# Layer 1's queries as three groups of block products, a product behind each stage of a head, and weights' sums by adding transfers

## The chip, the cores and the metric

The kernel runs on one NeuronCore of a Trainium2 chip. The metric is device time in microseconds, the median of three runs: 1967.92 us for the kernel before (1966.67 to 1968.24). All timelines below are of one profiled execution.

## What is computed

512 tokens of width 1024 pass two layers, each a gated feed-forward (width 2816), a mixer and a second feed-forward. Layer 0's mixer is a gated causal convolution of width 3 beside four heads of attention to 256 memory tokens; layer 1's is eight heads of causal attention with forget gates (the fox heads) beside four memory heads. All is float32. The lines of the reference that the change bears on are these:

```python
proj = h @ a_w_in[i]                      # layer 0: gates, u and qm
qm = proj[..., 3 * CONV_DIM:].reshape(b, s, MEM_HEADS, MEM_HEAD_DIM)
y_mem = memory_attention(qm, mk, mv)
x = x + jnp.concatenate([y_tok, y_mem], axis=-1) @ a_w_out[i]
...
proj = h @ b_w_q[j]                       # layer 1: q and qm, 12 tiles of 128 columns
q = proj[..., :FOX_WIDTH].reshape(b, s, FOX_HEADS, FOX_HEAD_DIM)
qm = proj[..., FOX_WIDTH:].reshape(b, s, MEM_HEADS, MEM_HEAD_DIM)
y_tok = forgetting_attention(q, k_sh, v_sh, c_sh)
y_mem = memory_attention(qm, mk, mv)
```

`memory_attention` is a softmax of q k / sqrt(128) over 256 memory tokens, times v.

## The kernel before

Activations lie transposed, as eight tiles of 128 features by 512 tokens. A float32 product is made of three TensorE products of rounded halves (`mm3`, L223, L226, L227): each operand is split into a high part `hi` (ScalarE, a copy that rounds, L129 for weights and L231 for activations) and a low part `lo` (VectorE, the rest, L130 and L232).

**Two ways to multiply.** A plain projection (`project`) makes one tile of 128 outputs with 8 x 3 matmuls of 512 columns. A block product group (`group`) takes a 2 x 2 block of weights (two output tiles by two halves of the inputs, each block 512 x 256) and of activations (feature halves by token halves; `Quad` makes the combinations of activations that it needs) and makes four output tiles with seven products instead of eight. Each product is 24 matmuls of 256 columns that accumulate in a PSUM bank. The products are called B11, T1, T2, B21, T3, B22 and T4; `Rows` takes their results apart into tiles. A group whose input statistics are still under way is called with `first`, and makes these statistics behind its second product.

**The weights** are one stream of units in program order (`Weights`, `W`). A unit is 128 x 1024: loaded eight units ahead on SyncE's queue (SP), split two units ahead, and used once. A block of seven units is made from five raw tiles, since three of its units are sums of blocks: raw[4] = a21 + a22 and raw[3] = a11 + a21 are loaded with a second, accumulating load on GpSimd's queue (POOL, L100), and raw[0] += raw[4] and raw[1] += raw[0] are made in place on VectorE (L138) behind the splits of the second and the fourth unit. PIECE says which raw tile each unit reads. Raw tiles lie in 5 buffers `wr` and 3 buffers `ws`, split ones in 4 `wh` and 4 `wl`.

**The mixers.** In layer 0 the four memory heads' queries are one group (`first`), and then the convolution's first three groups are drawn, two products at a time, beside the stages of the heads: `scores` (TensorE, reductions on VectorE, exponentials on ScalarE, `normalise` on VectorE), `turn` (eight transposes on TensorE, then splits) and `values`. In layer 1 each of the twelve query tiles is a plain projection, drawn by `pipeline` three heads ahead, the fox heads' first four beside the memory heads and the other four behind the out-projection. PSUM has eight banks: four `mm`, three `seeded` and one `aux`; while `spread` is set, which it is throughout layer 1's mixer, plain tiles rotate through seven.

**What sets the order.** A scheduler orders the instructions of each engine when the program is built, by its own estimates of durations and by priorities in program order; each engine then runs its own in that fixed order. Loads on SP stand in the order that the code writes. An instruction that waits holds up all behind it on its engine.

Of the kernel before, what the change touches and what calls it, by code (L numbers as in the profile page):

```python
# [12 lines left out]
ALU = mybir.AluOpType  # L13
# [15 lines left out]
MH = 4  # L29
# [10 lines left out]
class Weights:  # L40
# [5 lines left out]


    LOAD, SPLIT = 8, 2

# [15 lines left out]

    def block(self, ap):

        w = ap.shape[1] // 4
        item = {"ap": [ap[:, i * w : (i + 1) * w] for i in range(4)], "w": w, "raw": [None] * 5}
        self.units += [(item, q) for q in range(7)]  # L70
# [42 lines left out]
    def begin(self):  # L113

        i = self.split
        self.split += 1
        item, q = self.units[i]
        self.load_to(i + 1)
        if q is None:
            step, raw, w = item["step"], item["raw"], item["ap"].shape[1]  # L120
        else:
            step = w = item["w"]
            raw = item["raw"][self.PIECE[q]]
        hi, lo = self.tile("wh", F32R), self.tile("wl", F32R)
        self.parts[i] = (hi, lo)
        for a in range(0, w, step):
            c = slice(a, min(a + step, w))
            yield (
                self.nc.scalar.activation(hi[:, c], raw[:, c], AF.Copy),  # L129
                self.nc.vector.tensor_tensor(  # L130
                    out=lo[:, c], in0=raw[:, c], in1=hi[:, c].bitcast(F32), op=ALU.subtract
                ),
            )

        for at, to, of in ((1, 0, 4), (3, 1, 0)):
            if q == at:
                r = item["raw"]
                self.nc.vector.tensor_tensor(out=r[to][:, :w], in0=r[to][:, :w], in1=r[of][:, :w], op=ALU.add)  # L138
# [13 lines left out]
def model(ctx: ExitStack, tc: tile.TileContext, A, out):  # L152
# [45 lines left out]

    def bank(tag="mm"):
        if tag == "mm" and spread[0]:  # L200
            tag = ["mm"] * 4 + ["seeded"] * 3
            tag = tag[taken[0] % 7]
            taken[0] += 1
        return ppool.tile([P, T], F32, tag=tag, name=name(tag), bufs=BANKS[tag])

    def prime(x):

        spread[0] = False
        for b in [bank("seeded") for _ in range(BANKS["seeded"])]:
# [157 lines left out]
    chunks(A["mkv"][1])  # L367
    plan_ffn(0)
    for i in range(4):
        W.block(A["ain"][i])  # L370
    chunks(A["wout"][0, :2])
# [4 lines left out]
    plan_ffn(2)  # L376
    chunks(A["wqm"])
    chunks(A["wq"][:2])
    chunks(A["wout"][1, :2])
    chunks(A["wq"][2:])  # L380
    W.add(A["wf"], (KD * NH,))
# [172 lines left out]
    def ffn(n, x, quads, st, cols, last=None, begin=None):  # L554


        nst, nxt = Stats(), [c() for c in cols]
        new = list(x)
        hid = {}
        def halves(t):  # L560
# [88 lines left out]
    class OutProj:  # L649
# [7 lines left out]
        def run(self, d, upto, ahead=Weights.SPLIT):  # L657
# [4 lines left out]
            if d not in self.ps:  # L662
                self.ps[d] = bank()
            for k in range(self.done[d], upto):
# [209 lines left out]

    def queries(q, nd, st):

        wait = []

        def project_(h):
            wait.append((h, project(nd, mid=st.step1 if h == 1 else None)))  # L880
            if h:
                for i, ps in wait:
                    q[i] = scaled(ps, SCALE, st.row)
                wait.clear()

        return project_

    X0 = [keep(x) for x in X]
    store(KD)
    q, ym, yt, acc, gc = {}, {}, [None] * KD, {}, {}  # L890

    def query(row, i, t):
        q[2 * row + i] = parts()
        split(t, *q[2 * row + i])

# [39 lines left out]
    def gated(ch):  # L935
        def done(row, i, t):
            yt[ch + 2 * row + i] = parts()
            split(t, *yt[ch + 2 * row + i])

        return Rows(done, lambda row, i: acc[ch + 2 * row + i])  # L940

# [15 lines left out]

    for _ in group(quads.quads, Rows(query, lambda row, i: st.row, SCALE), begin):
        pass
    more = channels(0)  # L960

    def products(n):
        for _ in range(n):
            next(more)


    products(2)
    for i in range(MH + 2):
        if i >= 2:
            values(i - 2)  # L970
        if 0 < i <= MH:
            turn(i - 1)
        if i < MH:
            scores(i)
        products(2)
    for _ in more:
        pass
    X = [x() for x in X0]
# [8 lines left out]
    store(KD)  # L987
    X, st, (nd,) = ffn(2, X, quads.quads, st2, [lambda: Normed(V_MIX + 8)])

    spread[0] = True  # L990

    q, ym, Q, kvn = {}, {}, {}, Normed(V_KV)

    def fox_query():
        Q[len(Q)] = scaled(project(nd), SCALE, st.row)

    pipeline(MH, 3, queries(q, nd, st), *mem_heads(q, *mem_back(1), ym), [fox_query] * 4)
    for k in range(KD):
        kvn.add(k, X0[k]("t"))
    OutProj(X, ym, MH).finish()  # L1000
    for _ in range(4):
        fox_query()

# [229 lines left out]
def laid_out(a):  # L1233
# [55 lines left out]
    for c in (0, 4):  # L1289
        rows += [(8 + c, 16 + c), (10 + c, 18 + c), (c, c + 2)]  # L1290
    r0, r1 = (t[[i for r in rows for i in (r[h], r[h] + 1)]] for h in range(2))
    g["ain"] = blocks(
        *(two(v, 0) for v in (r0[:, :, :KP], r0[:, :, KP:], r1[:, :, KP:], r1[:, :, :KP]))
    )

# [8 lines left out]
    tk, tq = tiles(kvf[:, :D]), tiles(a["b_w_q"][0])  # L1304
    g["wqm"] = pairs(tq[NH:], 2)
    g["wk"], g["wq"] = pairs(tk, 2), pairs(tq[:NH], 2)
    vec = np.zeros((P, NVEC), f)
# [37 lines left out]
```

## Time and profile before

| what | value |
|---|---|
| median of three runs | 1967.92 us (1966.67 to 1968.24) |
| the profiled execution's time | 1968.88 us |
| its span | 1967.1 us, mean granted clock 0.995 |
| layer 0's query group, first part | 411.6 to 436 us |
| layer 0's heads with products beside them | 436 to 486 us |
| layer 1's entry, its memory heads | 1330 us, 1340 to 1382 us |
| VectorE in-place sums L138 | 102 in the whole kernel, 1.22 us each |

The page gives for each engine its busy time, and for groups of instructions the line, the engine, output and input tiles, their count, busy time and mean; a row of the timeline gives the start and the duration in us, and in square brackets how long the engine had been idle and what released it. `<-` points from the output to its inputs. The lines that matter stand in the prediction.

### The profile page before, as it was taken

Reading aid. Unit: us, or ns where it says so; the run is one execution under the profiler, and the core shown is the slowest. Engines: PE = TensorE matmul, PEld = TensorE weight load, DVE = VectorE, ACT = ScalarE, POOL = GpSimd, SP = SyncE. Lnnn points to the kernel's source line nnn. Section 1 sums busy time; section 2 is a strip of 40 time slices with the busy share of each in tenths; the row PEclk is TensorE's granted clock in tenths of the full one; section 3 lists DMA queues with packets and bytes.
Section 4 is the critical chain, followed back from the end, with each engine's and each line's share of the span. In section 5 each row is a group of like instructions: output and inputs, shape, how many; then the busy total and the mean of one; then the engine's idle time right before and its main releaser. Section 6 shows DMA issues by size and latency. Waiting matters only on the chain.

```text
span 1967.1 us, 31607 instructions
## 1 busy us (share of the span) xinstructions
PE 1942.0 (99%) x12845; PEld 1786.9 (91%) x12845; DVE 1437.4 (73%) x1998; ACT 976.5 (50%) x1434; POOL 102.8 (5%) x138
## 2 busy tenths in 40 slices
PE   8899999999999999999999999999999999999998
PEld 7899999999998998989899898988878889989896
DVE  7976667798787975767887576777546688757674
ACT  7653444566455652535565253545335575525353
POOL 0000000000000000000000000000001100000000
PEclk9899999999999999999999999999999999999999
DMA  8875566665664673657467365432322237637441
GB/s 294 229 218 154 135 158 153 176 170 142 183 177 123 165 197 100 173 138 181 150 177 190 97 174 140 131 127 96 127 93 69 76 98 194 192 100 179 131 116 43
DMA packets 89010, 293.32 MB, mean 149 GB/s; under 512 B 10016, under 2 KB 12192, under 8 KB 88864
## 3 DMA queue, kind: packets, MB, share of 16 engines
q1 hardware_dynamic: 74176, 237.82, 37.1%
q0 software_dynamic: 14688, 53.48, 17.0%
q8 instruction: 100, 1.64, 0.3%
q14 instruction: 46, 0.38, 0.1%
HBM read 280.78 MB, written 10.49 MB: 148 GB/s over the span
## 4 chain that ended last, share of the span: by engine, by line
PE 95%; DVE 3%; ACT 1%; DMA 1%; issue 1%; SPq 0%; DVEq 0%; ACTq 0%
PE mm L223 19%; PE mm L226 19%; PE mm L227 19%; PE seeded L223 12%; PE seeded L227 12%; PE seeded L226 12%; DMA wr<-in_mkv 1%; DVE wl L130 1%; DVE s L232 0%; ACT wh L129 0%; PE mm L1118 0%; DVE t L251 0%; DVE wr L138 0%; PE seeded L1118 0%; PE mm L756 0%
## 5 line engine op out<-in xcount | busy, mean ns | idle before, releaser
L129 ACT ACTIVATE wh<-wr 128x1024 fp32r<-128x1024 f32 (+2 forms) x422 | 437.0, 1038 | 699.5 <-PE mm L226 352.8
L223 PE MATMUL mm<-s,wh 128*128 128x256 f32 (+1 forms) x2236 | 734.3, 329 | 1.1 <-ACT s L235 1.1
L226 PE MATMUL mm<-s,wh 128*128 128x256 f32 (+1 forms) x2236 | 734.4, 328 | 0.7 <-DVE s L232 0.5
L227 PE MATMUL mm<-s,wl 128*128 128x256 f32 (+1 forms) x2236 | 733.7, 328 | 0.9 <-DVE wl L130 0.8
L130 DVE TENSOR_TENSOR wl<-wr,wh 128x1024 fp32r<-128x1024 f32 (+2 forms) x422 | 503.4, 1194 | 173.9 <-ACT wh L129 172.2
L223 PE MATMUL seeded<-s,wh 128*128 128x256 f32 (+1 forms) x1748 | 507.3, 290 | 0.3 <-ACT t L454 0.3
L227 PE MATMUL seeded<-s,wl 128*128 128x256 f32 (+1 forms) x1748 | 506.2, 290 | 0.0
L226 PE MATMUL seeded<-s,wh 128*128 128x256 f32 (+1 forms) x1748 | 506.1, 290 | 0.0
L223 PEld LDWEIGHTS mm<-s,wh 128*128 128x128 f32 x2236 | 426.3, 191 | 38.7 <-ACT s L235 1.8
L226 PEld LDWEIGHTS mm<-s,wh 128*128 128x128 f32 x2236 | 426.3, 191 | 38.6 <-DVE s L232 1.3
L227 PEld LDWEIGHTS mm<-s,wl 128*128 128x128 f32 x2236 | 426.2, 191 | 38.2 <-DVE wl L130 1.3
L223 PEld LDWEIGHTS seeded<-s,wh 128*128 128x128 f32 x1748 | 335.1, 192 | 4.8 <-ACT t L454 0.5
L227 PEld LDWEIGHTS seeded<-s,wl 128*128 128x128 f32 x1748 | 335.1, 192 | 4.4
L226 PEld LDWEIGHTS seeded<-s,wh 128*128 128x128 f32 x1748 | 335.1, 192 | 4.1
L628 DVE SCALAR_TENSOR_TENSOR t<-mm,r 128x512 f32<-128x512 f32 x96 | 66.1, 688 | 172.3 <-PE mm L227 172.3
L129 ACT ACTIVATE wh<-ws 128x1024 fp32r<-128x1024 f32 x102 | 108.2, 1061 | 137.3 <-PE mm L226 59.2
L100 POOL DMA_DIRECT2D ws<-in_gu x88 | 76.5, 870 | 1237.0 <-DMA ws<-in_gu 337.6
L232 DVE TENSOR_TENSOR s<-t,s 128x512 fp32r<-128x512 f32 (+1 forms) x204 | 126.7, 632 | 4.1 <-ACT s L231 4.0
L130 DVE TENSOR_TENSOR wl<-ws,wh 128x1024 fp32r<-128x1024 f32 x102 | 124.2, 1218 | 1.3 <-ACT wh L129 0.5
L231 ACT ACTIVATE s<-t 128x512 fp32r<-128x512 f32 (+1 forms) x204 | 112.4, 577 | 14.9 <-DVE t L306 7.8
L457 DVE TENSOR_TENSOR t<-seeded,t 128x512 f32<-128x512 f32 x94 | 64.7, 688 | 36.3 <-PE seeded L227 36.2
L631 DVE TENSOR_TENSOR s<-s,t 128x512 f32<-128x512 f32 (+1 forms) x97 | 66.4, 685 | 2.6
(183 smaller groups left out, 1412.1 us busy)
## 6 DMA issues: line engine op xcount, KB each, us to landing
wr<-in_gu SPq DMA_DIRECT2D x132, 512.0 KB, 4.0
ws<-in_gu SPq DMA_DIRECT2D x88, 512.0 KB, 4.5
ws<-in_gu POOLq DMA_DIRECT2D x88, 512.0 KB, 6.3
wr<-in_dn SPq DMA_DIRECT2D x64, 512.0 KB, 4.4
wr<-in_dn SPq DMA_DIRECT2D x32, 384.0 KB, 4.0
wr<-in_wout SPq DMA_DIRECT2D x24, 512.0 KB, 4.4
wr<-in_ain SPq DMA_DIRECT2D x21, 512.0 KB, 4.9
kept<-s SPq DMA_DIRECT2D x32, 256.0 KB, 3.1
```

The costliest lines, as they stand in the source:

```text
L100: self.nc.gpsimd.dma_start(out=t[:, :w], in_=more, accum_op=ALU.add)
L129: self.nc.scalar.activation(hi[:, c], raw[:, c], AF.Copy),
L130: self.nc.vector.tensor_tensor(out=lo[:, c], in0=raw[:, c], in1=hi[:, c].bitcast(F32), op=ALU.subtract),
L223: i = nc.tensor.matmul(ps, wh, xh, start=first, stop=more, skip_group_check=more)
L226: nc.tensor.matmul(ps, wh, xl, start=False, stop=more, skip_group_check=more)
L227: nc.tensor.matmul(ps, wl, xh, start=False, stop=last or more, skip_group_check=more)
L231: nc.scalar.activation(hi, src, AF.Copy)
L232: nc.vector.tensor_tensor(out=lo, in0=src, in1=hi.bitcast(F32), op=ALU.subtract)
L457: nc.vector.tensor_tensor(out=out, in0=a, in1=b, op=ALU.add)
L628: nc.vector.scalar_tensor_tensor(out=t[:, c], in0=ps[:, c], scalar=-0.5, in1=st.row[:, c], op0=ALU.mult, op1=ALU.mult)
L631: nc.vector.tensor_tensor(out=y[:, c], in0=y[:, c], in1=t[:, c], op=ALU.add)
```

## The change

Four things change.

1. Layer 1's twelve query tiles become three block groups (`g["bin"]`, in the order memory heads, fox heads 0 to 3, fox heads 4 to 7). Feed-forward 2 ends in `Quads` instead of `Normed`; the first group makes the statistics. X is stored (`X1`) and loaded again behind the groups, as in layer 0, and the inputs of keys and values are loaded (`kvn`) there too. All queries come ahead of the out-projection. The out-projection's tiles stay on the four `mm` banks, also where it is continued late in the mixer; `spread` is set only behind layer 1's memory heads.
2. Both mixers draw products beside the heads by one new function, `beside`, one product between stages.
3. The second and the third block of each mixer (`moved`) have their two sums made by adding transfers from SBUF to SBUF on POOL's queue, issued behind the splits of the first and the fourth unit.
4. Small shared helpers (`head`, `by_rows`) take the place of repeated code.

```diff
-    def block(self, ap):
+    def block(self, ap, moved=False):
...
+        r = item["raw"]
+        for at, to, of in ((0, 0, 4), (3, 1, 0)) if item["moved"] else ((1, 0, 4), (3, 1, 0)):
+            if q == at and item["moved"]:
+                self.nc.gpsimd.dma_start(out=r[to][:, :w], in_=r[of][:, :w], accum_op=ALU.add)
+            elif q == at:
                 self.nc.vector.tensor_tensor(out=r[to][:, :w], in0=r[to][:, :w], in1=r[of][:, :w], op=ALU.add)
...
-    def bank(tag="mm"):
-        if tag == "mm" and spread[0]:
-            tag = ["mm"] * 4 + ["seeded"] * 3
-            tag = tag[taken[0] % 7]
+    def bank(tag=None):
+        if tag is None:
+            tag = "seeded" if spread[0] and taken[0] % 7 > 3 else "mm"
             taken[0] += 1
...
     for i in range(4):
-        W.block(A["ain"][i])
+        W.block(A["ain"][i], i in (1, 2))
...
-    chunks(A["wqm"])
-    chunks(A["wq"][:2])
+    for i in range(3):
+        W.block(A["bin"][i], i in (1, 2))
     chunks(A["wout"][1, :2])
-    chunks(A["wq"][2:])
...
-                self.ps[d] = bank()
+                self.ps[d] = bank("mm")
...
+    def head(t, q, h):
+        q[h] = parts()
+        split(t, *q[h])
+
+    def queries(quads, st, q, first):
+
+        done = lambda row, i, t: head(t, q, 2 * row + i)
+        for _ in group(quads, Rows(done, lambda row, i: st.row, SCALE), first):
+            pass
+
+    def beside(more, scores, turn, values):
+        def products(n):
+            for _ in range(n):
+                next(more, None)
+
+        products(1)
+        scores(0)
+        products(2)
+        for h in range(MH):
+            turn(h)
+            if h + 1 < MH:
+                products(1)
+                scores(h + 1)
+                products(1)
+                values(h)
+                products(1)
+            else:
+                products(2)
+                values(h)
+        for _ in more:
+            pass
...
-    for _ in group(quads.quads, Rows(query, lambda row, i: st.row, SCALE), begin):
-        pass
-    more = channels(0)
-
-    def products(n):
-        for _ in range(n):
-            next(more)
-
-    products(2)
-    for i in range(MH + 2):
-        if i >= 2:
-            values(i - 2)
-        if 0 < i <= MH:
-            turn(i - 1)
-        if i < MH:
-            scores(i)
-        products(2)
-    for _ in more:
-        pass
+    queries(quads.quads, st, q, begin)
+    beside(channels(0), scores, turn, values)
...
-    X, st, (nd,) = ffn(2, X, quads.quads, st2, [lambda: Normed(V_MIX + 8)])
+    X, st, (quads,) = ffn(2, X, quads.quads, st2, [lambda: Quads(V_MIX + 8)])
+
+    X1 = [keep(x) for x in X]
+    store(KD)
+    q, ym, Q, kvn = {}, {}, {}, Normed(V_KV)
+
+    def fox_queries():
+        for h in (0, MH):
+            done = lambda row, i, t: head(t, Q, h + 2 * row + i)
+            g = group(quads.quads, Rows(done, lambda row, i: st.row, SCALE))
+            for _ in UNITS:
+                next(g, None)
+                yield
+
+    stages = mem_heads(q, *mem_back(1), ym)
+    queries(quads.quads, st, q, st.step1)
+    beside(fox_queries(), *stages)
+    X = [x() for x in X1]
+    for k in range(KD):
+        kvn.add(k, X0[k]())
+    OutProj(X, ym, MH).finish()
 
     spread[0] = True
-
-    q, ym, Q, kvn = {}, {}, {}, Normed(V_KV)
-
-    def fox_query():
-        Q[len(Q)] = scaled(project(nd), SCALE, st.row)
-
-    pipeline(MH, 3, queries(q, nd, st), *mem_heads(q, *mem_back(1), ym), [fox_query] * 4)
-    for k in range(KD):
-        kvn.add(k, X0[k]("t"))
-    OutProj(X, ym, MH).finish()
-    for _ in range(4):
-        fox_query()
```

Line numbers of the changed kernel are a little higher: the splits of weights are L130 and L131, the accumulating load L101, the adding transfer L141, the copies L457, the exponentials L749.

**Place one: POOL in layer 0's mixer.** In the kernel before, the accumulating loads of the convolution's blocks follow one another (ws339 and ws348 are of the second block in the stream, ws358 and ws367 of the third, ws377 of the fourth):

```order
L100 DMA ws339_4313<-in_ain 128x1024
L100 DMA ws348_4478<-in_ain 128x1024
L100 DMA ws358_4636<-in_ain 128x1024
L100 DMA ws367_4774<-in_ain 128x1024
L100 DMA ws377_5011<-in_ain 128x1024
L100 DMA ws386_5183<-in_ain 128x1024
```

In the changed kernel, the same place reads:

```order
L101 DMA ws339_4313<-in_ain 128x1024
L101 DMA ws348_4478<-in_ain 128x1024
L101 DMA ws358_4636<-in_ain 128x1024
L141 DMA wr340_4316<-ws339_4313 128x1024
L101 DMA ws367_4774<-in_ain 128x1024
L141 DMA wr345_4436<-wr340_4316 128x1024
L101 DMA ws377_4981<-in_ain 128x1024
L141 DMA wr359_4639<-ws358_4636 128x1024
L101 DMA ws386_5153<-in_ain 128x1024
L141 DMA wr364_4742<-wr359_4639 128x1024
```

Each sum of a moved block (wr340, wr345, then wr359, wr364) stands behind an accumulating load of a later tile. In layer 1's mixer the first two sums likewise stand behind a load each (ws1089, ws1098).

**Place two: ScalarE in the same stretch.** wh360 is the split of the second block's summed unit (raw wr340, for its third product), wh365 and wh368 are later units, s_ are splits of the query tiles, and the exponentials belong to head 0. Before:

```order
L129 ACTIVATE wh360_4676<-wr340_4316 128x1024
L231 ACTIVATE s_427_4622<-t_422_4551 128x512
L129 ACTIVATE wh362_4707<-wr345_4436 128x1024
L454 ACTIVATE seeded_436_4704<-mm_435_4675 128x512
L231 ACTIVATE s_429_4627<-t_423_4553 128x512
L129 ACTIVATE wh365_4770<-ws348_4478 128x1024
L231 ACTIVATE s_431_4666<-t_425_4587 128x512
L454 ACTIVATE t_438_4738<-mm_437_4706 128x512
L231 ACTIVATE s_433_4671<-t_426_4589 128x512
L129 ACTIVATE wh368_4803<-wr345_4436 128x1024
L745 ACT_TABLE_LOAD
L745 ACTIVATE t_442_4743,su_440_4741<-mm_441_4742,nm_439_4740 128x256 x2
```

After:

```order
L130 ACTIVATE wh360_4676<-wr340_4316 128x1024
L234 ACTIVATE s_429_4628<-t_423_4553 128x512
L130 ACTIVATE wh362_4737<-wr345_4436 128x1024
L234 ACTIVATE s_431_4666<-t_425_4587 128x512
L457 ACTIVATE seeded_436_4704<-mm_435_4675 128x512
L130 ACTIVATE wh365_4770<-ws348_4478 128x1024
L234 ACTIVATE s_433_4671<-t_426_4589 128x512
L749 ACT_TABLE_LOAD
L749 ACTIVATE t_440_4709,su_438_4707<-mm_439_4708,nm_437_4706 128x256 x2
L749 ACTIVATE t_442_4718,su_438_4707<-mm_441_4717,nm_437_4706 128x256 x2
L457 ACTIVATE t_445_4768<-mm_444_4736 128x512
L457 ACTIVATE seeded_446_4801<-seeded_436_4704 128x512
```

The summed unit's split keeps its place, but reads what POOL's transfer leaves; the copy `seeded_436` of the first product's result stands one split later, and wh368, the unit of the second sum, has moved from ahead of head 0's exponentials to behind them.

**Place three: VectorE in the same stretch.** wl361 and wl369 are the low parts of the two summed units, nm_ the reductions of head 0's scores, rs_ and the two rows behind it its normalising, and s_449 the low part of head 0's turned tile. Before:

```order
L130 TENSOR_TENSOR wl363_4708<-wr345_4436,wh362_4707 128x1024
L232 TENSOR_TENSOR s_430_4628<-t_423_4553,s_429_4627 128x512
L138 TENSOR_TENSOR wr345_4436<-wr345_4436,wr340_4316 128x1024
L232 TENSOR_TENSOR s_432_4667<-t_425_4587,s_431_4666 128x512
L740 TENSOR_REDUCE nm_439_4740<-mm_441_4742 128x2
L232 TENSOR_TENSOR s_434_4672<-t_426_4589,s_433_4671 128x512
L740 TENSOR_REDUCE nm_439_4740<-mm_443_4751 128x2
L130 TENSOR_TENSOR wl366_4771<-ws348_4478,wh365_4770 128x1024
L130 TENSOR_TENSOR wl369_4804<-wr345_4436,wh368_4803 128x1024
L721 RECIPROCAL rs_445_4764<-su_440_4741 128x4
L723 TENSOR_SCALAR t_442_4743<-t_442_4743,rs_445_4764 128x256 x2
L723 TENSOR_SCALAR t_444_4752<-t_444_4752,rs_445_4764 128x256 x2
```

After:

```order
L744 TENSOR_REDUCE nm_437_4706<-mm_439_4708 128x2
L235 TENSOR_TENSOR s_432_4667<-t_425_4587,s_431_4666 128x512
L744 TENSOR_REDUCE nm_437_4706<-mm_441_4717 128x2
L131 TENSOR_TENSOR wl363_4738<-wr345_4436,wh362_4737 128x1024
L235 TENSOR_TENSOR s_434_4672<-t_426_4589,s_433_4671 128x512
L131 TENSOR_TENSOR wl366_4771<-ws348_4478,wh365_4770 128x1024
L725 RECIPROCAL rs_443_4730<-su_438_4707 128x4
L727 TENSOR_SCALAR t_440_4709<-t_440_4709,rs_443_4730 128x256 x2
L727 TENSOR_SCALAR t_442_4718<-t_442_4718,rs_443_4730 128x256 x2
L131 TENSOR_TENSOR wl369_4822<-wr345_4436,wh368_4821 128x1024
L235 TENSOR_TENSOR s_449_4809<-mm_447_4803,s_448_4808 128x512
```

The sum L138 is gone from between the query tiles' splits, and wl369 has moved from ahead of head 0's normalising to between it and the split of the turned tile.

More of the change, by code (lines that the diff above doesn't have):

```diff
@@ L64, in add @@
         assert at == ap.shape[1]
-    def block(self, ap):
+    def block(self, ap, moved=False):
         w = ap.shape[1] // 4
-        item = {"ap": [ap[:, i * w : (i + 1) * w] for i in range(4)], "w": w, "raw": [None] * 5}
+        item = {"ap": [ap[:, i * w : (i + 1) * w] for i in range(4)], "w": w, "raw": [None] * 5, "moved": moved}
         self.units += [(item, q) for q in range(7)]
@@ L133, in begin @@
             )
-        for at, to, of in ((1, 0, 4), (3, 1, 0)):
-            if q == at:
-                r = item["raw"]
+        if q is None:
+            return
+        r = item["raw"]
[3 more added lines that the diff above has]
+            elif q == at:
                 self.nc.vector.tensor_tensor(out=r[to][:, :w], in0=r[to][:, :w], in1=r[of][:, :w], op=ALU.add)
@@ L206, in prime @@
     def prime(x):
-        spread[0] = False
         for b in [bank("seeded") for _ in range(BANKS["seeded"])]:
@@ L558, in ffn @@
         new = list(x)
+        spread[0] = False
         hid = {}
@@ L872, in model @@
     )
[L875 to L886, printed above, removed]
+    def head(t, q, h):
[25 more added lines that the diff above has]
+            pass
     X0 = [keep(x) for x in X]
@@ L890, in model @@
     q, ym, yt, acc, gc = {}, {}, [None] * KD, {}, {}
-    def query(row, i, t):
-        q[2 * row + i] = parts()
-        split(t, *q[2 * row + i])
     r2 = small.tile([P, T], F32, tag="r2", name="r2", bufs=1)
@@ L935, in gated @@
     def gated(ch):
[L936 to L940, printed above, removed]
+        return Rows(lambda row, i, t: head(t, yt, ch + 2 * row + i), lambda row, i: acc[ch + 2 * row + i])
     def channels(ch):
@@ L1290, in laid_out, with by_rows @@
         rows += [(8 + c, 16 + c), (10 + c, 18 + c), (c, c + 2)]
[L1291 to L1294, printed above, removed]
+    def by_rows(t, rows):
+        r0, r1 = (t[[i for r in rows for i in (r[h], r[h] + 1)]] for h in range(2))
+        return blocks(
+            *(two(v, 0) for v in (r0[:, :, :KP], r0[:, :, KP:], r1[:, :, KP:], r1[:, :, :KP]))
+        )
+    g["ain"] = by_rows(t, rows)
     def outw(w):
@@ L1304, in laid_out @@
     tk, tq = tiles(kvf[:, :D]), tiles(a["b_w_q"][0])
-    g["wqm"] = pairs(tq[NH:], 2)
-    g["wk"], g["wq"] = pairs(tk, 2), pairs(tq[:NH], 2)
+    g["wk"] = pairs(tk, 2)
+    g["bin"] = by_rows(tq, [(8, 10), (0, 2), (4, 6)])
     vec = np.zeros((P, NVEC), f)
```

## The prediction

> **What bounds the kernel now.** The page comes first: one core, its span, what each engine is busy, and the chain of work that ended last.
>
> ```profile
> span 1967.1 us, 31607 instructions
> PE 1942.0 (99%) x12845; PEld 1786.9 (91%) x12845; DVE 1437.4 (73%) x1998; ACT 976.5 (50%) x1434; POOL 102.8 (5%) x138
> PE 95%; DVE 3%; ACT 1%; DMA 1%; issue 1%; SPq 0%; DVEq 0%; ACTq 0%
> ```
>
> TensorE is the bound: a matmul less is worth its issue interval, and every other engine matters only where TensorE waits for it. So the second view is that of TensorE's waits, and the third the busy time in the stretches that the change touches: layer 0's group and heads (436 to 486), the two stage entries (985, 1330) and layer 1's heads (1340).
>
> ```profile
> PE aux L261 <- ACT t L231: 6.4, 1, 6.4
> PE mm L223 <- DVE s L232: 1.7, 2, 1.4
> ...
> 411.60:436.00 24.40, 24.16 (x196) 23.48 (x195) 24.19 (x37) 15.82 (x22) 0.86 (x1) 1.00 0.78 229
> 436.00:468.00 32.00, 30.61 (x246) 29.71 (x245) 30.93 (x52) 24.94 (x54) 2.60 (x3) 1.00 0.62 146
> 468.00:486.40 18.40, 18.11 (x127) 17.12 (x126) 15.30 (x26) 9.85 (x20) 0.88 (x1) 0.91 0.53 136
> 985.00:1005.00 20.00, 19.76 (x159) 19.08 (x158) 20.00 (x29) 14.42 (x19) 0.86 (x1) 1.00 0.58 155
> 1330.00:1340.00 10.00, 10.00 (x45) 8.23 (x45) 8.33 (x10) 4.27 (x6) 0.00 (x0) 1.00 0.46 163
> 1340.00:1382.00 42.00, 42.00 (x226) 36.06 (x225) 29.84 (x55) 23.69 (x56) 0.00 (x0) 1.00 0.26 87
> ```
>
> The columns after the stretch are PE, PEld, DVE, ACT, POOL, then the granted clock. Layer 1's heads lose nothing today: TensorE is busy 42.00 of 42.00 us. Layer 0's lose 1.39 us (30.61 of 32.00) in a single gap, and VectorE has almost no slack there (24.19 of 24.40, then 30.93 of 32.00).
>
> **What goes, and what comes for it.** Layer 1's twelve query tiles are plain projections today, each 8 x 3 matmuls of 512 columns. Two starts of such matmuls that lie ten apart, and then the first 256-column matmuls of two products in a row (24 apart):
>
> ```profile
> 1327.79 0.39 PE L226 MATMUL mm<-s,wh 128*128 128x512 f32 x1
> ...
> 1330.06 0.40 PE L227 MATMUL mm<-s,wl 128*128 128x512 f32 x1
> ...
> 440.31 0.28 PE L223 MATMUL seeded<-s,wh 128*128 128x256 f32 x1
> ...
> 443.19 0.28 PE L223 MATMUL mm<-s,wh 128*128 128x256 f32 x1
> ```
>
> From start to start that is 2.27 / 10 = 0.227 us and 2.88 / 24 = 0.120 us. So 12 x 24 x 0.227 = 65.3 us goes, and 3 groups x 7 products x 24 x 0.120 = 60.5 us comes: **-4.8 us**. Its entry takes the form that layer 0's and the feed-forward stages' entries have, whose rows above show 0.24 us idle each (24.16 of 24.40, 19.76 of 20.00) where layer 1's shows none: **+0.2**.
>
> In layer 0 the products are spread out so that one stands behind each stage of a head. The gap of 1.39 us stood before the scores of a head, with the turn directly ahead of it:
>
> ```profile
> 465.07 1.04 PE L756 MATMUL mm<-cst,t 128*128 128x128 f32 x8
> 467.50 0.38 PE L223 MATMUL mm<-s,s 128*128 128x256 f32 x1 [1.39 <-DVE s L232]
> ```
>
> In the new order a product stands between a turn and the next scores, so this wait has 2.9 us of cover. With it goes the lowered clock behind it (0.91 over 18.4 us: 18.4 x 0.09 = 1.7 us). **-3.1**.
>
> A sentence of the Trainium skill stands against that last figure: "TensorE: Matmul & The Clock Gate" (Why this matters for your kernels) puts the harm to the clock at idle gaps over about 3 us; by it the 1.39 us gap would have cost no clock, and the change would get 1.4 here rather than 3.1. The row with 0.91 disagrees with the page, and the measurement decides.
>
> Without any new wait the sum is 1968.9 - 4.8 + 0.2 - 3.1 = **1961.2** on the profiled execution's scale (1968.88 us for a span of 1967.1), about 1 less on the scale of the median.
>
> **The sums by adding transfers.** A group needs two sums of raw weights, r0+=r4 and then r1+=r0. Today VectorE makes them (L138), and in the second and third group of each mixer an accumulating transfer on POOL's queue does now. VectorE is relieved of 8 x 1.2 us. The price is latency, and here are the rows for it: the sum in layer 0's second group and what stands around it, on VectorE, POOL and ScalarE.
>
> ```profile
> L138 DVE TENSOR_TENSOR wr<-wr,ws 128x1024 f32<-128x1024 f32 x51 | 62.4, 1224 | 1.4
> ...
> 428.38 1.22 DVE L130 TENSOR_TENSOR wl<-wr,wh 128x1024 fp32r<-128x1024 f32 x1
> 432.53 1.22 DVE L138 TENSOR_TENSOR wr<-wr,ws 128x1024 f32<-128x1024 f32 x1
> ...
> 429.45 0.86 POOL L100 DMA_DIRECT2D ws<-in_ain  x1 [20.64 <-DMA ws<-in_ain]
> ...
> 433.86 1.06 ACT L129 ACTIVATE wh<-wr 128x1024 fp32r<-128x1024 f32 x1 [4.52 <-DVE wr L138]
> 436.29 0.58 ACT L454 ACTIVATE seeded<-mm 128x512 f32<-128x512 f32 x1
> 441.15 1.28 ACT L745 ACT_TABLE_LOAD   x1
> 442.45 0.47 ACT L745 ACTIVATE t<-mm,nm 128x256 f32<-128x256 f32 x1
> ...
> 444.63 1.14 DVE L723 TENSOR_SCALAR t<-t,rs 128x256 f32<-128x256 f32 x4
> ```
>
> The sum must not start before the first unit's split has read r0 (VectorE, 428.38 + 1.1 = 429.5). On POOL it stands directly behind the next group's accumulating load, which is at 429.45 and leaves POOL free at 430.31. So the transfer is issued at about 430.3 where VectorE's sum was ready at 433.66: it has 3.4 us. No row shows an accumulating transfer within SBUF. The nearest are the accumulating loads of the same 512 KB: the one at 429.45, then two issued 1.2 us apart, alone by the first and then the second.
>
> ```profile
> ws<-in_ain POOLq DMA_DIRECT2D x1, 512.0 KB, 6.3
> ...
> ws<-in_gu POOLq DMA_DIRECT2D x1, 512.0 KB, 6.1
> ...
> ws<-in_gu POOLq DMA_DIRECT2D x1, 512.0 KB, 8.4
> ```
>
> The second one takes 8.4 us because it queues behind the first. The new sum is issued 0.9 us behind another accumulating load, which is that case, so I take 8.4: it lands at L = 430.3 + 8.4 = **438.7**. The bounds are 433.7 (as ready as now) and 438.7; alone it would be 436.6.
>
> By a page of the Trainium skill it would be the low end: "DMA: Bandwidth & Descriptors" (Anatomy of one DMA, SWDGE path) fits 2.0 us + bytes/436e3 per us, that is an estimate of 3.2 us for 512 KB, a landing at 433.5 and no wait. The trace's 6.1 to 8.4 us for accumulating loads of that size disagree with the fit.
>
> What L does is seen from ScalarE's order: the split of the summed unit stands ahead of another split, of the copy that product 3 accumulates onto, and of head 0's exponentials; all of them wait with it. From the rows: split to end of copy is 433.86 to 436.87, 3.0 us, and one more 512-column split (0.5) now lies between, so product 3 can start at L + 3.5 = 442.2, where TensorE wants it at 440.31. Head 0's normalised exponentials come after one more weight split and one more split (1.5), the table load, exponentials and normalising (441.15 to 445.77, 4.6): L + 9.6 = 448.3. TensorE wants the turn at 443.19. So it is 5.1 late.
>
> The second sum (r1+=r0) waits for VectorE's split of the summed r0, which stands behind two splits and two reductions: about L + 5.7. It also has another accumulating load ahead of it on POOL, so again 8.4: L2 = L + 14.1 = 452.8. In VectorE's order its unit's split (0.95 on ScalarE, 1.1 on VectorE) stands ahead of the split of head 0's turned tile, and the second half of head 1's scores takes that tile's bank: possible at L2 + 2.75 = 455.6. TensorE without waits is there at 443.19 + 0.86 (turn) + 2.88 (product) + 0.72 (half the scores) = 447.65. So by then the layer is **7.9 us** late, the 5.1 included. Layer 1 has the same orders, load and sum adjacent on POOL included: **+8**. The third group's sums follow half a stage later; between 0 and 2.9 for layer 0, where the fourth sum has a load ahead of it, and 0 to 0.5 for layer 1, taken as 2 together. Sum: 7.9 + 8 + 2 = **+18**.
>
> **Smaller edits.** Feed-forward 2's last downs make operands of block products where they made normalised tiles, as feed-forwards 0 and 1 do without loss. X is stored and fetched again, and the inputs of keys and values are fetched later: -0 to +3, taken as 0. The out-projection keeps to four banks, so the last head's turned tiles share one: 0 to +3, taken as 0. Layer 1's VectorE work grows to about that of layer 0's heads (30.93 of 32.00), but the eight sums are gone from it: 0 to +2, taken as 0.
>
> **Rivals.** (a) *The transfer is quick*: within SBUF it lands by about 434, all waits above vanish, and the sum is 1961.2, that is **1960** as a median: faster. It turns on this one latency: below 3.4 us no wait, and above, each us costs about one in each layer. For it: nothing is fetched from HBM. Against it: the nearest rows take 6.1 or more. This is also what the fit on the Trainium skill's page "DMA: Bandwidth & Descriptors" would give. (b) *Not queued but alone*: 6.3 us for each of the two, so L = 436.6, L2 = L + 12 = 448.6, and the scores' bank is free at 451.4: 3.7 us late per layer; 1961.2 + 7.5 + 1 = 1969.7, **1969** as a median: no difference. (c) *The waits add up*: the third group's too (+3.4), a lowered clock behind each long wait (0.09 over 18 us, 1.7 us twice), and the tail's banks (+3): 1961.2 + 16 + 3.4 + 3.4 + 3 = **1987**. (d) *It doesn't do what it says*: relieved or not, VectorE stays as busy, and layer 0 keeps its 3.1 us; that adds 3 to each case above (1981 to the forecast, 1963 to (a)) and changes no sign, so it has no chance of its own.
>
> **How the numbers follow.** The forecast: 1961.2 + 18 = 1979.2, on the median's scale **1978**, chance 0.44; (c) 0.18; (b) and its neighbourhood 0.16; (a) 0.22. The range 1960 to 1988 takes in all of them save the ends, the forecast's own range is 1972 to 1983. About 0.2%, 3.9 us, is what a measurement of this kernel can tell from no change. Faster by more (below 1964.0): 0.22, that is (a). Within: 0.14, most of (b). Slower (above 1971.9): 0.64.
>
> **What would show it.** In the profile of the changed kernel: the adding transfers' time to landing (6 to 8 us right, under 4 wrong); TensorE's waits for the exponentials' normalising before head 0's turn and for VectorE's split before head 1's scores, some 8 us in each mixer; ScalarE idle at the summed unit's split with the transfer as releaser; the 1.39 us wait gone. A transfer of 3 us, or TensorE busy throughout both mixers, would make the prediction wrong, and so would sums that another order on ScalarE lets pass.

## The result, and the profile after

The changed kernel takes **1983.91 us** (median, 1980.87 to 1985.33), the kernel before 1967.99 in the same session: 1.0081 times as long, 95% interval 1.0069 to 1.0093. It is slower, by 15.9 us. The profiled execution of the changed kernel took 1984.88 us. Of its page, the span, the engines' busy time and the chain that ended last by engine:

```profile
span 1983.1 us, 32232 instructions
...
PE 1942.6 (98%) x13061; PEld 1795.3 (91%) x13061; DVE 1459.0 (74%) x2053; ACT 998.0 (50%) x1472; POOL 114.9 (6%) x152
...
PE 88%; DVE 5%; DMA 3%; issue 2%; ACT 1%; SPq 0%; DVEq 0%; ACTq 0%; POOL 0%; POOLq 0%
```

The view of TensorE's waits (source, total us, times, longest):

```profile
PE mm L226 <- DVE s L235: 9.8, 4, 3.4
PE aux L264 <- ACT t L234: 6.4, 1, 6.4
PE mm L760 <- DVE t L727: 4.6, 2, 2.3
```

TensorE's share of the chain that ended last fell from 95% to 88%, and transfers and VectorE took it over. Of the waits, the 6.4 us one is from the start of the kernel and was there before; the first row was 1.7 us and the third is new. In layer 0 they stand where the prediction put them, in the timeline of TensorE (start, duration, instruction, idle time before it and its releaser):

```profile
441.34 0.39 PE L226 MATMUL seeded<-s,wh 128*128 128x256 f32 x1 [0.99 <-ACT seeded L457]
...
446.77 1.25 PE L760 MATMUL mm<-cst,t 128*128 128x128 f32 x8 [2.29 <-DVE t L727]
...
454.97 0.39 PE L226 MATMUL mm<-s,s 128*128 128x256 f32 x1 [3.38 <-DVE s L235]
```

These are product three, head 0's turn, and the second half of head 1's scores: 0.99 + 2.29 + 3.38 = 6.7 us. The last head's scores wait another 1.28 us. What made these three late is read from the chain of waits in the same stretch (start, duration, what), here without its short issue steps:

```profile
421.32 7.16 DMA ws<-in_ain
...
429.83 7.82 DMA wr<-ws
...
437.75 1.07 ACT wh L130
...
438.85 1.22 DVE wl L131
440.07 0.60 DVE s L235
440.67 0.60 DVE nm L744
441.27 0.60 DVE s L235
441.87 0.60 DVE nm L744
442.47 1.13 DVE wl L131
443.60 0.61 DVE s L235
444.22 7.76 DMA wr<-wr
...
452.00 1.06 ACT wh L130
```

TensorE is not in it at all. The path is a load, the first sum's transfer, the split of the summed unit on ScalarE and VectorE, VectorE's queue up to the split of the next unit, the second sum's transfer, and its split again. Each of these two transfers takes 7.8 us where VectorE's add took 1.2. The waits also cost clock; the windows (TensorE, its loads, VectorE, ScalarE and POOL busy, then the granted clock) show 0.93 and 0.92 behind them in the two mixers:

```profile
444.00:470.00 26.00, 20.33 (x150) 19.51 (x150) 16.03 (x29) 14.68 (x34) 2.62 (x3) 0.93 0.75 181
1384.00:1405.00 21.00, 18.13 (x133) 17.57 (x132) 15.11 (x28) 14.48 (x34) 0.86 (x1) 0.92 0.28 77
```

That is about 26 x 0.07 + 21 x 0.08 = 3.5 us on top of the idle time. Narrower windows show that each of the two is a single stretch of 3.4 us at half the clock, and that the 0.91 of the kernel before, which the prediction read over 18.4 us, is one such stretch too (first the kernel before, then the changed one, each time with the 3.4 us ahead of it):

```profile
465.82:469.24 3.42, 1.74 (x13) 1.30 (x12) 3.42 (x7) 1.63 (x4) 0.00 (x0) 1.00 0.59 157
469.24:472.65 3.41, 3.41 (x17) 3.18 (x16) 3.41 (x6) 2.11 (x9) 0.00 (x0) 0.50 0.07 24
...
452.29:455.71 3.42, 0.74 (x6) 0.74 (x7) 2.62 (x3) 3.42 (x5) 0.88 (x1) 1.00 0.76 183
455.71:459.12 3.41, 3.41 (x19) 3.41 (x18) 3.27 (x5) 2.60 (x11) 0.00 (x0) 0.50 0.96 235
1384.13:1387.55 3.42, 0.71 (x7) 0.48 (x5) 3.13 (x7) 3.29 (x9) 0.00 (x0) 1.00 0.00 0
1387.55:1390.96 3.41, 3.25 (x15) 3.28 (x16) 3.41 (x6) 2.42 (x9) 0.00 (x0) 0.50 0.00 0
```

Layer 1 has waits of 2.30 and 2.25 us at the turn and the second half of the scores, none at product three, and one of 2.87 us behind the third sum. Its first two transfers, 1.6 and 2.1 us behind a load (0.7 and 2.0 in layer 0), landed after 6.8 and 6.6 us.

### The profile page after: what moved, and what is told of

Read it like the earlier page. It is cut to its first block, busy times and chain, and to the rows that moved or that the text cites. A ratio compares the mean times of both kernels' runs of the same rounds, so it can differ in the third digit from the quotient of the medians.

```text
span 1983.1 us, 32232 instructions
## 1 busy us (share of the span) xinstructions
PE 1942.6 (98%) x13061; PEld 1795.3 (91%) x13061; DVE 1459.0 (74%) x2053; ACT 998.0 (50%) x1472; POOL 114.9 (6%) x152
## 3 DMA queue, kind: packets, MB, share of 16 engines
q8 instruction: 102, 1.67, 0.3%
## 4 chain that ended last, share of the span: by engine, by line
PE 88%; DVE 5%; DMA 3%; issue 2%; ACT 1%; SPq 0%; DVEq 0%; ACTq 0%; POOL 0%; POOLq 0%
PE mm L226 19%; PE mm L229 19%; PE mm L230 18%; PE seeded L226 11%; PE seeded L229 10%; PE seeded L230 10%; DVE wl L131 1%; DMA wr<-ws 1%; DVE s L235 1%; DMA wr<-in_mkv 1%; ACT wh L130 1%; DMA wr<-wr 1%; DMA ws<-in_ain 0%; PE mm L1126 0%; DVE t L254 0%
## 5 line engine op out<-in xcount | busy, mean ns | idle before, releaser
L130 ACT ACTIVATE wh<-wr 128x1024 fp32r<-128x1024 f32 (+2 forms) x425 | 440.2, 1038 | 668.8 <-PE mm L229 344.3
L226 PE MATMUL mm<-s,wh 128*128 128x256 f32 (+1 forms) x2288 | 746.3, 327 | 3.4 <-DVE s L235 2.9
L229 PE MATMUL mm<-s,wh 128*128 128x256 f32 (+1 forms) x2288 | 746.7, 326 | 1.0 <-DVE s L235 0.7
L230 PE MATMUL mm<-s,wl 128*128 128x256 f32 (+1 forms) x2288 | 746.0, 326 | 0.8 <-DVE wl L131 0.8
L131 DVE TENSOR_TENSOR wl<-wr,wh 128x1024 fp32r<-128x1024 f32 (+2 forms) x425 | 506.8, 1194 | 186.9 <-ACT wh L130 185.3
L226 PEld LDWEIGHTS mm<-s,wh 128*128 128x128 f32 x2288 | 436.5, 191 | 40.4 <-issue 3.1
L229 PEld LDWEIGHTS mm<-s,wh 128*128 128x128 f32 x2288 | 436.6, 191 | 38.0 <-DVE s L235 1.5
L230 PEld LDWEIGHTS mm<-s,wl 128*128 128x128 f32 x2288 | 436.5, 191 | 37.1 <-DVE wl L131 1.4
L226 PEld LDWEIGHTS seeded<-s,wh 128*128 128x128 f32 x1768 | 339.9, 192 | 3.6 <-ACT seeded L457 1.2
L229 PEld LDWEIGHTS seeded<-s,wh 128*128 128x128 f32 x1768 | 340.0, 192 | 1.7
L632 DVE SCALAR_TENSOR_TENSOR t<-mm,r 128x512 f32<-128x512 f32 (+1 forms) x97 | 66.5, 685 | 166.1 <-PE mm L230 166.1
L130 ACT ACTIVATE wh<-ws 128x1024 fp32r<-128x1024 f32 x108 | 114.5, 1061 | 142.1 <-PE mm L229 61.2
L101 POOL DMA_DIRECT2D ws<-in_gu x88 | 76.5, 869 | 1241.3 <-DVE wl L131 360.3
L235 DVE TENSOR_TENSOR s<-t,s 128x512 fp32r<-128x512 f32 (+1 forms) x220 | 135.4, 625 | 4.3 <-ACT s L234 4.3
L131 DVE TENSOR_TENSOR wl<-ws,wh 128x1024 fp32r<-128x1024 f32 x108 | 131.5, 1217 | 2.3 <-ACT wh L130 1.4
L234 ACT ACTIVATE s<-t 128x512 fp32r<-128x512 f32 (+1 forms) x220 | 120.4, 571 | 24.7 <-DVE t L526 10.6
```

Source lines behind the costliest of these rows:

```text
L101: self.nc.gpsimd.dma_start(out=t[:, :w], in_=more, accum_op=ALU.add)
L131: self.nc.vector.tensor_tensor(out=lo[:, c], in0=raw[:, c], in1=hi[:, c].bitcast(F32), op=ALU.subtract),
L226: i = nc.tensor.matmul(ps, wh, xh, start=first, stop=more, skip_group_check=more)
L229: nc.tensor.matmul(ps, wh, xl, start=False, stop=more, skip_group_check=more)
L230: nc.tensor.matmul(ps, wl, xh, start=False, stop=last or more, skip_group_check=more)
L234: nc.scalar.activation(hi, src, AF.Copy)
```

## The experiments

Ten kernels were run: e1 to e4 in one session (the kernel before at 1967.99 us), e5 to e8 in a second (1967.39) and e9 and e10 in a third (1967.33). Each median has an interval of some 1.8 to 3 us to both sides, so that between two sessions a difference under some 2.5 us shows nothing by the times alone. The profiles are finer. The changed kernel and the ten runs have the same number of TensorE instructions, so the start of an instruction in one profile can be subtracted from the start of the one at the same place in the other. Over stretches that an edit does not touch the difference stays the same within 0.2 us; only the first 100 us vary, by up to 3.5 us. (The kernel before has fewer instructions in layer 1's mixer alone and is compared from both ends.)

**One: all sums back on VectorE (e1).** The rest of the change stays.

```diff
-        W.block(A["ain"][i], i in (1, 2))
+        W.block(A["ain"][i], False)
...
-        W.block(A["bin"][i], i in (1, 2))
+        W.block(A["bin"][i], False)
```

> All sums of weights back on VectorE, the rest of the change kept. Theory A (the transfers' latency holds up the summed unit's split and all behind it on ScalarE and VectorE): TensorE's seven waits in the two mixers' heads (7.9 us in layer 0, 7.4 us in layer 1 in the changed kernel's profile) and some 4 us of lowered clock behind them go: 1963 to 1968. Rival B (VectorE is full in the new order of heads and products, and the transfers relieve it): 1984 or more, with TensorE waiting for VectorE's splits in the heads. Rival C (the loss is the later fetch of X, the inputs of keys and values, and the four banks): 1980 to 1984.

Measured: 1966.75 us, 0.9995 of the kernel before (0.9985 to 1.0004). The transfers cost 1983.91 - 1966.75 = 17.2 us. By equal instructions, 8.7 us of it lie in layer 0's query group and heads, 7.8 in layer 1's and 1.2 at the forget gates' product. The window that held most of layer 0's waits is free of them, at full clock:

```profile
444.00:470.00 26.00, 26.00 (x209) 25.48 (x208) 23.46 (x40) 16.66 (x37) 1.73 (x2) 1.00 0.52 122
```

So A holds: the transfers are the loss, and neither B nor C is. VectorE is not quite free, though. Just outside this window TensorE waits 0.22 and 0.90 us for VectorE's splits, and in layer 1 1.44 us. The rest of the change, without the transfers, gains nothing that shows.

**Two: the sums as adds on GpSimd (e2).** One line, at the transfers' place:

```diff
-                self.nc.gpsimd.dma_start(out=r[to][:, :w], in_=r[of][:, :w], accum_op=ALU.add)
+                self.nc.gpsimd.tensor_tensor(out=r[to][:, :w], in0=r[to][:, :w], in1=r[of][:, :w], op=ALU.add)
```

> The eight moved sums as adds that GpSimd computes, at the places where the transfers were issued. The trace has adds of 128 x 128 there at 0.46 us, so 1024 columns are estimated at 3.7 us: ready at about 433.6 in layer 0 (429.8 + 3.7) where the transfer landed at 437.65, which is when VectorE's sum was ready in the kernel before. Theory A: nearly all the waits go, 1963 to 1970, whichever engine adds. Rival B: VectorE is as relieved as with the transfers; slower than the sums on VectorE is impossible, so this is below the first run. Rival C: 1980 to 1984.

Measured: 1974.13 us, 1.0033 (1.0020 to 1.0046). Better than the transfers, yet 7.4 us worse than VectorE's own sums, which the expectation had called impossible. By equal instructions, layer 0's heads are 4.0 us longer than in e1 and layer 1's 3.6. The timelines of POOL and of VectorE in this run show why:

```profile
428.94 2.72 POOL L141 TENSOR_TENSOR wr<-wr,ws 128x1024 f32<-128x1024 f32 x1
...
428.77 3.18 DVE L526 SCALAR_TENSOR_TENSOR t<-t,r 128x256 f32<-128x256 f32 x2
...
434.32 0.76 DVE L526 SCALAR_TENSOR_TENSOR t<-t,r 128x256 f32<-128x256 f32 x2
```

The add itself is quicker than estimated, 2.7 us for 3.7. But two VectorE instructions that read two tiles from SBUF take 3.18 us together beside it, where such a pair takes 0.76 a little later: VectorE stands still until GpSimd's add is done. So this add relieves VectorE of 1.2 us and takes 2.4 from it. Over the whole run, VectorE's 2053 instructions are busy 1472.9 us, where the same 2053 of the changed kernel take 1459.0. The Trainium skill says as much in "SBUF — State Buffer" (Who interferes with whom): a VectorE instruction with two SBUF inputs contends with a GpSimd instruction that reads SBUF, and the contention is an exclusive lock. The trace agrees.

**Three and four: one block's sums each (e3, e4).** Transfers for the second block alone (`i == 1` in place of `i in (1, 2)`), and for the third alone (`i == 2`).

> Only the second block of each mixer has its sums by transfers, the third has them on VectorE. Theory A: the waits before product three, the first turn and the second head's scores stay in both mixers (6.7 and 4.5 us, and their clock), the later ones (1.3 and 2.9 us) go: 1974 to 1981. Rival B: 1984 or more. Rival C: 1980 to 1984.

> Only the third block of each mixer has its sums by transfers. Theory A: only the later waits stay (1.3 us in layer 0, 2.9 us in layer 1, and some clock): 1967 to 1973. Rival B: 1984 or more. Rival C: 1980 to 1984.

Measured: 1982.74 us (1.0077, 1.0062 to 1.0092) and 1966.72 us (0.9994, 0.9985 to 1.0004). The second block's transfers are nearly the whole loss; the third's alone cost nothing that shows. The first is 1.7 us above what A gave and lies in the range of C, which e1 has ruled out; the second is a little below its range. That e4 equals e1 is a balance: by equal instructions layer 0's heads are 2.4 us longer in it, and layer 1's 1.6 shorter, since the 1.44 us wait of e1 is gone there. The transfers of the sums, with the median from issue to landing at the end of the row, in e3:

```profile
wr<-ws POOLq DMA_DIRECT2D x2, 512.0 KB, 7.5
wr<-wr POOLq DMA_DIRECT2D x2, 512.0 KB, 7.5
```

and in e4:

```profile
wr<-ws POOLq DMA_DIRECT2D x2, 512.0 KB, 6.6
wr<-wr POOLq DMA_DIRECT2D x2, 512.0 KB, 4.8
```

The 6.6 is the median of 8.7 us in layer 0, behind a load, and 4.5 in layer 1, alone.

**Five: each sum ahead of the next load (e5).** All transfers stay; the sums and the accumulating loads of these blocks keep the order in which the code issues them. Instructions and order on all other engines are the same as in the changed kernel; on POOL, the sum changes places with the load ahead of it.

```diff
-                self.nc.gpsimd.dma_start(out=r[to][:, :w], in_=r[of][:, :w], accum_op=ALU.add)
+                self.pin(self.nc.gpsimd.dma_start(out=r[to][:, :w], in_=r[of][:, :w], accum_op=ALU.add))
...
-    W = Weights(nc, wpool)
+    W = Weights(nc, wpool); W.pin = tc.keep_in_program_order
```

> The changed kernel with all its adding transfers; only on POOL's queue each sum stands ahead of the next accumulating load instead of behind it, and every other engine has the same instructions in the same order. In the profiles a sum that lay alone in the queue landed after 4.5 to 5.0 us, one behind a load after 7.0 to 8.6. Theory A1 (the place behind the load makes the sum late): the first sum lands at 430.0 + 4.5 = 434.5 instead of 437.65; product three does not wait, head 0's turn about 1 us, the second head's scores not at all: 1967 to 1972. Theory A2 (a transfer is too slow for a sum that is needed one unit later, wherever it stands): 1978 to 1984.

Measured: 1972.58 us, 1.0029 (1.0020 to 1.0038): 11.3 us less than the changed kernel from POOL's order alone (10 by the two ratios), and 0.6 us above the range that A1 gave. The transfers of this run:

```profile
wr<-ws POOLq DMA_DIRECT2D x4, 512.0 KB, 4.8
wr<-wr POOLq DMA_DIRECT2D x4, 512.0 KB, 4.8
```

and of the chain of waits in layer 0:

```profile
427.93 4.79 DMA wr<-ws
...
432.82 1.07 ACT wh L130
```

Ahead of the load the sum takes 4.8 us, and the summed unit's split starts at 432.82 instead of 437.75. It is now the loads behind the sums that are late, with medians of 7.8 and 7.7 us to landing in place of 6.1 and 6.6, but what they bring is needed later. A1 holds in kind, though the second head's scores, which were not to wait at all, wait 1.22 us. What is left of the loss is 1972.58 - 1966.75 = 5.8 us, since 4.8 us are still more than there is time for: this profile shows waits of 0.51, 1.22 and 1.79 us in layer 0's heads and of 0.37, 0.31 and 2.88 in layer 1's, and three stretches of 3.4 us at half the clock.

**Six: layer 0's heads in the old order (e6).** As e1, with `beside(channels(0), scores, turn, values)` replaced by the loop of the kernel before, two products at a time.

> All sums on VectorE (as in the first run, 1966.75), and layer 0's heads in the old order, two products at a time; layer 1 keeps the new one. If a product behind each stage takes away the wait of 1.4 us in layer 0 and its lowered clock, as the prediction had it (3.1 us), undoing it costs that: 1968.5 to 1970.5. If the order of the stages is worth nothing in layer 0: 1966 to 1967.5.

Measured: 1966.81 us, 0.9997 (0.9988 to 1.0006), as good as e1. The window of layer 0's stretch in this run:

```profile
425.00:490.00 65.00, 63.32 (x492) 61.55 (x492) 58.34 (x94) 40.60 (x81) 4.34 (x5) 0.97 0.56 140
```

and of e1:

```profile
425.00:490.00 65.00, 63.88 (x510) 62.28 (x509) 60.01 (x98) 41.08 (x82) 5.01 (x6) 1.00 0.58 149
```

In these two executions the new order saves 0.6 us of idle time and one stretch of half the clock, 1.7 us; by equal instructions layer 0's heads are 2.1 us longer in e6. The medians, of two sessions, show none of it. In layer 0, e6 is the kernel before, so what it has left of the change is layer 1's groups with the four banks and the later fetches that come with them. Together these are worth 1967.39 - 1966.81 = 0.6 us, which is within the noise; what the groups alone are worth it does not show.

**Seven: seven banks again (e7).** As e1, and

```diff
-                self.ps[d] = bank("mm")
+                self.ps[d] = bank()
```

> All sums on VectorE, and the out-projection's tiles rotate through seven banks again where spread is set. In the first run's profile TensorE idles four times for 0.07 to 0.35 us, 0.85 us together, in the last fox head, where the kernel before does not. If the four banks are the cause, with the clock behind it: 1964 to 1966. If the last head is slow for another reason: 1966 to 1967.5.

Measured: 1963.82 us, 0.9981 (0.9973 to 0.9990), 2.9 us below e1 and slightly faster than expected. By equal instructions the last fox heads are 2.3 us shorter than in e1, but the forget gates' product waits longer and takes 1.2 of it back; so the four banks cost 2.3 us there, of which the idle times are 0.85, and the rest of the 2.9 is within what two sessions differ by. e1's timeline of the last fox head has these idle times, which are gone in e7:

```profile
1576.45 0.44 PE L226 MATMUL seeded<-s,s 128*128 128x384 f32 x1 [0.23 <-ACT s L234]
...
1577.25 0.44 PE L1126 MATMUL mm<-cst,t 128*128 128x128 f32 x2 [0.35 <-DVE s L235]
...
1578.22 0.39 PE L226 MATMUL seeded<-s,s 128*128 128x256 f32 x1 [0.19 <-ACT s L234]
```

**Eight and nine: the late fetches (e8, e9).** e8 is e1 with the inputs of keys and values fetched ahead of X; e9 is e7 with X fetched at the start of the last fox group:

```diff
+            if h:
+                X[:] = [x() for x in X1]
             for _ in UNITS:
```

> All sums on VectorE, and the inputs of keys and values are fetched ahead of X behind layer 1's memory heads. In the first run's profile the forget gates' product waits 0.4 us for these inputs' splits. If the late fetch costs more than this wait shows: 1964 to 1966; if not, or if X is late in its place: 1966.5 to 1969.

> The kernel of the run with seven banks (all sums on VectorE), and X is fetched again at the start of the last fox group instead of behind it, so that the inputs of keys and values follow sooner. In that run's profile the forget gates' product waits 1.7 us for these inputs. If the fetch is what makes them late: 1961 to 1963. If the earlier fetch holds up the weights' loads behind it on SP's queue, for want of free tiles: 1965 to 1972.

Measured: e8 1971.25 us, 1.0020 (1.0012 to 1.0029), 4.5 us above e1. X is not what TensorE waits for there, as its timeline shows:

```profile
1418.46 0.40 PE L226 MATMUL aux<-s,wh 128*8 128x512 f32 x1 [1.50 <-ACT s L238]
...
1425.14 0.97 PE L226 MATMUL seeded<-wh,s 128*128 128x512 f32 x3 [0.91 <-ACT wh L130]
```

The forget gates' product (aux) now stands ahead of the out-projection's rest in TensorE's order, and its inputs, though fetched first, come later than it; the granted clock is 0.94 over these 30 us, in that run's windows from 1400 to 1430:

```profile
1400.00:1430.00 30.00, 26.32 (x104) 16.62 (x103) 14.61 (x22) 8.60 (x14) 0.00 (x0) 0.94 0.62 211
```

e9 takes 1964.16 us, 0.9985 (0.9976 to 0.9994), the same as e7 and between its two expected ranges. TensorE's waits in e7:

```profile
PE aux L226 <- ACT s L238: 1.7, 1, 1.7
...
PE mm L226 <- ACT s L238: 1.3, 1, 1.3
```

and in e9:

```profile
PE mm L760 <- ACT t L457: 1.1, 1, 1.1
PE mm L226 <- ACT s L238: 0.8, 1, 0.8
```

The forget gates' wait of 1.7 us is gone, but a turn in layer 1's heads now waits 1.1 us for a copy on ScalarE; by equal instructions the one stretch gets 1.9 us shorter than in e7 and the other 1.4 longer. What delays that copy was not tried.

**Ten: what is left in favour of transfers (e10).** Seven banks, transfers for the third block alone, each sum ahead of the next load.

> Seven banks for the out-projection, only the third block of each mixer with its sums by transfers, each ahead of the next load on POOL's queue (VectorE makes 4 sums, 4.9 us of its work, less than with all sums there). If the relief of VectorE is worth something once the transfers land in time: 1961 to 1963. If VectorE's sums cost nothing there, as the kernel with all of them on VectorE suggests: 1963 to 1965, as with seven banks alone.

Measured: 1961.95 us, 0.9974 (0.9965 to 0.9984). It beats the kernel before by 0.26% and the changed kernel by 1.1%, and is the best of the kernels here. Its interval and that of e7 overlap, so the times alone do not show that the four transfers have part in it. The profiles do show one: by equal instructions layer 1's heads are 1.7 us shorter than in e7, since the wait of 1.44 us for VectorE is gone as in e4, and the forget gates' stretch is 1.4 shorter (a wait of 0.28 in place of 1.67). Layer 0's heads are 0.7 longer: its first sum there took 7.0 us although it stood ahead of the load, and the last head's scores wait 1.59 us instead of 0.90.

```profile
475.63 0.39 PE L226 MATMUL mm<-s,s 128*128 128x256 f32 x1 [1.59 <-DVE s L235]
```

## Why the prediction was right, and where it was not

**The sign and the mechanism** were right. The first sum was to land at 438.7 and did at 437.65; head 0's turn was to be possible at 448.3 and came at 446.77; the second half of head 1's scores at 455.6, and came at 454.97. The choice of the 8.4 us row over the one of 6.3, since the sum stands right behind a load, is what e5 confirms: 7.8 us behind a load, 4.8 ahead of it. Neither of them is the 3.2 us of the fit on the Trainium skill's page "DMA: Bandwidth & Descriptors" (Anatomy of one DMA, SWDGE path), and rival (a), which needed less than 3.4, falls with it.

**That the price came out so near is in part luck.** +18 us was forecast for the transfers, and they cost 17.2 (the changed kernel against e1). But the +18 was idle time alone, 7.9 in layer 0, 8 in layer 1 and 2 for the third group. The profile has 6.7 and 4.6 us at the places forecast, and 1.3 and 2.9 behind the third group's sums: 15.4 in all, of which e1 keeps 2.6. The two stretches of lowered clock add 3.4, and the forget gates' product waits 1.2 us longer. Layer 1 was the most mis-sized: its first two transfers landed after 6.8 and 6.6 us, not 8.4; why they were quicker than layer 0's is not shown. Its whole stretch still came out at 7.8, by the third sum and the clock. The third group's sums, taken as 2, are worth 1.2 between the medians of the changed kernel and e3, which is within their ranges.

**Rival (c) described much of this.** It had the lowered clock (1.7 us twice), more from the third group, and the banks, and all three came. 1983.91 lies nearer to its 1987 than to the forecast of 1978, and just above the forecast's own range, 1972 to 1983.

**The sum without waits was mis-sized.** It said 1961.2, or 1960 as a median; e1, which is that case, takes 1966.75, and that is why the forecast fell 5.9 us short. By equal instructions layer 0's mixer is 2.1 us shorter in e1 than in the kernel before, where 3.1 was forecast, and layer 1's mixer is 0.8 us longer, where 4.8 - 0.2 = 4.6 was to be saved. The terms, roughly:

- The four banks, "0 to +3, taken as 0", cost 2.3 (the last fox heads, e1 against e7).
- Layer 1's heads, where nothing waited before and no new wait was counted besides the transfers'. With the sums on VectorE, a product waits for VectorE's split:

```profile
1371.31 0.35 PE L226 MATMUL mm<-s,wh 128*128 128x256 f32 x1 [1.44 <-DVE s L235]
```

"0 to +2, taken as 0" for VectorE's higher load there was 1.4; e4 and e10, with the third block's sums off VectorE, do not have this wait.

- Layer 0's heads, -3.1. The stretch of lowered clock went, 1.7, but of the idle time only some 0.5: waits of 0.22 and 0.90 us took the place of 1.39 and 0.29. The step that failed is the cover of "2.9 us" that a product gives to the wait behind a turn: for the last head the second half of the scores still waits for VectorE's split:

```profile
472.62 0.39 PE L226 MATMUL mm<-s,s 128*128 128x256 f32 x1 [0.90 <-DVE s L235]
```

- The late fetch, taken as 0, is a wait of 0.4 us in e1, of 1.6 in the changed kernel and of 1.7 in e7.

In layer 1 that leaves some 1.3 us that no run accounts for. In e10, which has the seven banks and hardly waits in layer 1, that mixer is 3.1 us shorter than in the kernel before. So most of the 4.8 us of matmuls is there to be had; that all of it is, is not shown.

**The clock.** The prediction took one stretch of lowered clock as the price of a wait of 1.39 us. The profiles show more of it. In each of the twelve, the stretches at half clock start whole multiples of 3.413 us apart (in the kernel before at 49.40, 73.29 and 469.24 us, 7 and 123 steps from the first). Cut into such steps between 90 and 1900 us, every step at full clock in which TensorE idled 1.9 us or more, seven in all, is followed by one at half clock. No step with 1.65 us or less is, and of five with 1.68 to 1.85 us three are. So in these kernels a step that was idle for about half of its length cost 1.7 us of clock, and a wait counted by what of it fell into one step. The 1.39 us had another 0.29 beside it in the same step. e4's wait of 1.88 us fell 1.30 into one step and 0.58 into the next, and cost no clock:

```profile
470.20:473.61 3.41, 2.11 (x18) 1.91 (x16) 2.11 (x4) 3.05 (x6) 0.00 (x0) 1.00 0.55 157
473.61:477.02 3.41, 2.83 (x23) 2.83 (x24) 3.41 (x6) 1.44 (x4) 0.67 (x1) 1.00 0.78 304
```

## What to carry to other kernels

An engine that is busy does not yet need relief: compare the latency of what takes its work over with the time until the result is read, not the two engines' busy times. Here 1.2 us of VectorE's work became 7.8 us on layer 0's path, and 4.8 of these were the operation and 3 its place in a queue that a scheduler had chosen. Where the result is read late enough, as in layer 1's third block, the same transfer took a wait away. When a block form saves a few matmuls, look at the banks, fetches and splits that come with it, for here they cost between a tenth and a half of the saving each.

## What was not expected of the hardware

An accumulating transfer of 512 KB within SBUF took 4.5 us alone in the queue, 4.8 to 5.5 us (once 7.0) just ahead of an accumulating load and 6.6 to 8.7 us within some 2 us behind one; such loads from HBM took a median of 6.1 to 6.6 us in the changed kernel. A GpSimd add of 128 x 1024 took 2.4 to 3.3 us, and a pair of VectorE instructions with two SBUF inputs beside one took 3.18 us instead of 0.76. The clock was lowered in steps of 3.413 us at one half, each behind a step in which TensorE had idled for about half of the time.
